# A hybrid decoder block in fp32 on one core: q, k and v leave the projection with channels on partitions, 512 tokens wide, DMAs set q's and k's parts down by head, and the units of mixer A come first

## The chip, the cores and the metric

One core of a Trainium2 chip. The metric is the device time of one execution in microseconds (us). Before the change it was 1175.13 us, the median of three runs (1171.29 to 1176.3).

## What is computed

One decoder layer over 1024 tokens (S) of width 1024 (D), fp32. Cut to what matters here:

```
h = rms_norm(x, g_attn_pre) * (1 + sc_a) + sh_a        # modulation from c @ w_ada
proj = h @ w_in                                        # 1024 -> 2304
qa, ka, va = 512, 128, 128 columns                     # A: 8 q heads, 2 kv heads of 64
qb, kb, vb = 512, 512, 512 columns                     # B: 8 heads of 64
qa, ka, qb, kb = partial_rope(..., cos, sin)           # first 16 of each 64, pairs (i, i+8)
oa = banded_attention(qa, ka, va, 127, sink)           # causal window of 128
ob = dilated_mixture_attention(qb, kb, vb)             # windows (128,1) (512,4) (2048,16)
y = concat(rms_norm(oa), rms_norm(ob)) @ w_out
x = x + gt_a * rms_norm(y, g_attn_post)
x = x + gt_m * rms_norm(sqrelu(h' @ w_up) @ w_down)    # h' from x as h above, 4096 wide
```

## The kernel before, in words

Each fp32 operand of a projection, score or output product is split into two fp32r numbers, hi (a rounded copy, on ScalarE, ACT) and lo (the rest, on VectorE, DVE, or on GpSimd, POOL). A product is three TensorE (PE) matmuls, hi x hi, hi x lo, lo x hi. Transposes are PE matmuls against an identity.

The projection runs in six units of 384 columns of w_in: units 0 to 3 are two B heads each (q, k, v of 128), units 4 and 5 one kv head of A each with its four q heads. For each of eight blocks of 128 tokens, `proj_mm` (L766, L767, L769) keeps a 128 x 128 piece of h (`hw`, hi and lo) as the stationary operand and moves 384 columns of w, over eight k of 128 channels: 48 tiles `pj` of 24 matmuls, tokens on partitions. `evac` (L666 to L758) then works a tile off: v split into hi and lo (L679, L684), the rotation on DVE (L695 to L699), q and k split (`sp`, `sk`, L706 to L712), both transposed by PE through the bank `px` (`pq` L719, `pk` L731), and the transposes copied out by ACT (`qt` L724, `kt` L745, L757). Unit 0 (`first_unit`, L788) has eight accumulators `acc` open at once while x and w_ada still arrive.

Attention goes by items: for B one head of two token blocks (32 items), for A four heads of one block (16). `s_b` (L996) makes a B item's scores `s_ps` in pieces of up to 256 keys (L1022), `s_a_` (L1055) A's (L1073). Masks, maxima, the exponential and its sum follow on DVE and ACT. `t_pv` (L1114) transposes probabilities (`pt_ps`, L1125, L1128, L1132), splits them (`ph`, ACT L1139 and DVE L1143) and multiplies with v into `o_ps` (L1156 to L1167), one PSUM bank `po`. The result `ot` is stored to DRAM (`o_dram`) by SyncE (SP, L1194 for B, L1214 for A). After all items `out_block` reads it back normed and multiplies with w_out (`y_ps`, L1373 to L1375; `load_wo`, L1234, brings and splits w_out). The MLP (`mlp_ps`, L1797 to L1799) follows.

The order on each engine comes from a scheduler in the program (`Sched`, L135): each step has an engine, an estimated duration, what it waits for, which buffers it takes and gives (`Res`), and a priority; steps are placed greedily when they could start. DMAs from SP are such steps, and SP carries them out in the order placed. For PE, `prefer` (L1949) ranks kinds: projection steps ("dense") ahead of attention steps while the projection leads attention by less than `LEAD` = 0.5 unit, behind them otherwise.

## Time and profile before

| what | value |
|---|---|
| median of three runs | 1175.13 us (1171.29 to 1176.3) |
| the profiled execution | 1175.14 us, its span 1173.3 us |
| granted TensorE clock | 0.993 of full speed |
| first transpose of q (unit 0) | 64.6 us |
| first y_ps matmul, first mlp_ps matmul | 436.4 us, 543.9 us |

The recorded lengths of matmuls overlap, since they are pipelined, so the distance from one start to the next is what a stream of them takes. A row such as `x4` stands for four alike in a run. A row of waits names the engine and the tile or line that waited, and after the arrow what released it; then come the sum in us, the number of waits and the longest.

### The profile page before, as it was taken

Reading aid. Unit: us, or ns where it says so; the run is one execution under the profiler, and the core shown is the slowest. Engines: PE = TensorE matmul, PEld = TensorE weight load, DVE = VectorE, ACT = ScalarE, POOL = GpSimd, SP = SyncE. Lnnn points to the kernel's source line nnn. Section 1 sums busy time; section 2 is a strip of 40 time slices with the busy share of each in tenths; the row PEclk is TensorE's granted clock in tenths of the full one; section 3 lists DMA queues with packets and bytes.
Section 4 is the critical chain, followed back from the end, with each engine's and each line's share of the span. In section 5 each row is a group of like instructions: output and inputs, shape, how many; then the busy total and the mean of one; then the engine's idle time right before and its main releaser. Section 6 shows DMA issues by size and latency. Waiting matters only on the chain.

```text
span 1173.3 us, 17394 instructions
## 1 busy us (share of the span) xinstructions
PE 1137.0 (97%) x6042; PEld 987.6 (84%) x6042; DVE 871.9 (74%) x1765; ACT 677.6 (58%) x1421; POOL 239.3 (20%) x295
## 2 busy tenths in 40 slices
PE   8999999999999999999899999999999999999996
PEld 7889999999988878887688888888888888888885
DVE  7876787776788896668969764499653796636998
ACT  7966676666666786666667524473225733246542
POOL 2053464554654451112000000000000000000002
PEclk9999999999999999999999999999999999999998
DMA  9712234132223224465485147922258411575103
GB/s 327 209 64 78 74 87 117 53 104 71 70 70 104 79 73 130 172 202 218 150 333 181 36 150 243 357 84 90 100 214 306 143 50 54 202 283 201 37 19 144
DMA packets 96488, 166.54 MB, mean 142 GB/s; under 512 B 11408, under 2 KB 48400, under 8 KB 96400
## 3 DMA queue, kind: packets, MB, share of 16 engines
q1 hardware_dynamic: 96400, 165.42, 42.0%
q8 instruction: 48, 0.79, 0.3%
q14 instruction: 40, 0.33, 0.1%
HBM read 137.08 MB, written 28.31 MB: 141 GB/s over the span
## 4 chain that ended last, share of the span: by engine, by line
PE 77%; DVE 11%; issue 4%; ACT 3%; POOL 1%; DMA 1%; DVEq 0%; POOLq 0%; SPq 0%; ACTq 0%
PE mlp_ps L1798 16%; PE mlp_ps L1799 16%; PE mlp_ps L1797 16%; PE pj L766 4%; PE pj L767 4%; PE pj L769 4%; PE s_ps L1022 3%; PE o_ps L1156 2%; PE pt_ps L1125 1%; DMA w_st<-in_w_in 1%; PE y_ps L1373 1%; PE y_ps L1375 1%; PE y_ps L1374 1%; PE s_ps L1073 1%; PE pt_ps L1128 1%
## 5 line engine op out<-in xcount | busy, mean ns | idle before, releaser
L1797 PE MATMUL mlp_ps<-hw 128*128 128x512 f32 x896 | 349.7, 390 | 1.1 <-ACT hw L1559 1.1
L1798 PE MATMUL mlp_ps<-hw 128*128 128x512 f32 x896 | 348.7, 389 | 1.1 <-DVE hw L1565 1.1
L1799 PE MATMUL mlp_ps<-hw 128*128 128x512 f32 x896 | 348.6, 389 | 0.0
L1797 PEld LDWEIGHTS mlp_ps<-hw 128*128 128x128 f32 x896 | 168.2, 188 | 36.9 <-ACT hw L1559 1.6
L1798 PEld LDWEIGHTS mlp_ps<-hw 128*128 128x128 f32 x896 | 168.2, 188 | 36.6 <-DVE hw L1565 1.4
L1799 PEld LDWEIGHTS mlp_ps<-hw 128*128 128x128 f32 x896 | 168.2, 188 | 34.9
L1568 DVE TENSOR_TENSOR hw<-w,hw 128x1024 fp32r<-128x1024 f32 x96 | 114.6, 1219 | 95.1 <-ACT hw L1561 93.0
L1561 ACT CAST hw<-w 128x1024 fp32r<-128x1024 f32 x96 | 97.4, 1046 | 129.9 <-PE mlp_ps L1799 93.2
L1897 POOL TENSOR_TENSOR st<-st,nhalf 128x1 f32<-128x1 f32 x8 | 7.7, 977 | 602.0 <-DVE st L1895 602.0
L766 PE MATMUL pj<-w_hl,hw 128*128 128x384 f32 x320 | 119.1, 372 | 0.0
L767 PE MATMUL pj<-w_hl,hw 128*128 128x384 f32 x320 | 108.7, 340 | 0.5 <-DVE w_hl L506 0.5
L769 PE MATMUL pj<-w_hl,hw 128*128 128x384 f32 x320 | 108.9, 340 | 0.0
L1561 ACT CAST hw<-u 128x1024 fp32r<-128x1024 f32 x48 | 48.6, 1052 | 64.6 <-PE mlp_ps L1799 64.6
L1143 DVE TENSOR_TENSOR ph<-pt_ps,ph 128x512 fp32r<-128x512 f32 (+1 forms) x110 | 68.9, 644 | 18.6 <-ACT ph L1139 18.0
L1568 DVE TENSOR_TENSOR hw<-u,hw 128x1024 fp32r<-128x1024 f32 x48 | 57.0, 1218 | 18.2 <-ACT hw L1561 18.2
L1139 ACT CAST ph<-pt_ps 128x512 fp32r<-128x512 f32 (+1 forms) x110 | 59.8, 562 | 12.9 <-PE pt_ps L1128 8.8
L1052 POOL TENSOR_SCALAR p_sb<-p_sb,den 128x128 f32<-128x128 f32 (+3 forms) x64 | 49.1, 773 | 87.4 <-DVE den L1050 49.8
L1855 DVE TENSOR_TENSOR yacc<-yacc,mlp_ps 128x512 f32<-128x512 f32 x96 | 62.2, 681 | 3.3 <-PE mlp_ps L1799 3.3
L767 PEld LDWEIGHTS pj<-w_hl,hw 128*128 128x128 f32 x320 | 61.0, 191 | 2.1 <-DVE w_hl L506 0.8
L766 PEld LDWEIGHTS pj<-w_hl,hw 128*128 128x128 f32 x320 | 60.7, 190 | 1.6 <-issue 0.5
L769 PEld LDWEIGHTS pj<-w_hl,hw 128*128 128x128 f32 x320 | 60.6, 189 | 0.0
L1047 ACT ACTIVATE p_sb<-p_sb,mn 128x128 f32<-128x128 f32 (+3 forms) x64 | 50.0, 782 | 17.4 <-DVE mn L1040 13.5
(206 smaller groups left out, 2201.0 us busy)
## 6 DMA issues: line engine op xcount, KB each, us to landing
hw<-s_dram SPq DMA_DIRECT2D x84, 512.0 KB, 4.4
wa_st<-in_w_ada SPq DMA_DIRECT2D x32, 512.0 KB, 4.2
w<-in_w_up SPq DMA_DIRECT2D x32, 512.0 KB, 5.1
w<-in_w_down SPq DMA_DIRECT2D x32, 512.0 KB, 7.5
s_dram<-hw SPq DMA_DIRECT2D x28, 512.0 KB, 4.5
x_sb<-in_x SPq DMA_DIRECT2D x16, 512.0 KB, 5.4
wa<-in_w_ada SPq DMA_DIRECT2D x32, 256.0 KB, 6.1
w_st<-in_w_in SPq DMA_DIRECT2D x32, 192.0 KB, 3.8
```

The lines of the kernel that those rows point to most:

```text
L766: T.matmul(ps, hw[:, tb, 0, t], w[:, 0], start=(k == 0), stop=False)
L767: T.matmul(ps, hw[:, tb, 0, t], w[:, 1], start=False, stop=False)
L769: T.matmul(ps, hw[:, tb, 1, t], w[:, 0], start=False, stop=(k == KC - 1))
L1047: A.activation(rec.p[qi], rec.p[qi], AF.Exp, bias=b["mn"][:, m:m + 1], scale=-1.0, accum_out=b["den"][:])
L1139: A.copy(b["ph"][:, 0, :w], b["pt"][:, :w])
L1143: V.tensor_tensor(b["ph"][:, 1, :w], b["pt"][:, :w], b["ph"][:, 0, :w].bitcast(F32), ALU.subtract)
L1561: A.copy(out[j][0], flat(src[j]))
L1568: V.tensor_tensor(out[j][1], flat(src[j]), out[j][0].bitcast(F32), ALU.subtract)
L1797: T.matmul(ps[m][:], sh, mh, start=starts and k == 0, stop=False, **kw)
L1798: T.matmul(ps[m][:], sh, ml_, start=False, stop=False, **kw)
L1799: T.matmul(ps[m][:], sl, mh, start=False, stop=k == 3, **kw)
L1855: e = op("DVE", t_dv(512), lambda: V.tensor_tensor(y(), y(), ps[m][:], ALU.add), [e, ml.e_y[tb, n]], gives=gives, prio=1)
```

## The change

**Operands swap in the projection.** w is stationary now, in blocks c = 0, 1, 2 of 128 columns for each unit, and `hw` moves, 512 tokens (x = 0, 1) as four blocks of 128 (L859, L860, L862): 36 tiles `pj` of 128 channels x 512 tokens with 24 matmuls each, 864 of 512 columns for 1152 of 384. The host orders w_in's columns so that c = 0 holds the 16 rotated rows of every q and k head of a unit (and for B nothing else, 128 rows in all), c = 1 more of q and k, c = 2 the rest and v. It comes as 36 tiles of 128 x 512 (L530) in place of 64 pieces (L484).

**Rotation and set-down.** Cos and sin stand in two tables of 128 x 1024 (`tabs`), made by `tables` with POOL fills and copies, PE transposes (`ptab`, L717) and ACT copies, once for A and again ahead of unit 2 for B. Block 0 is rotated by four DVE instructions over 512 tokens. Hi and lo of q and k go to `stage("hl")`, and DMAs on SP (L801) lay each head's 64 rows into `kt` and `qt`, of the one hi above lo, the other twice over: 18 DMAs for each half unit (u, x), 216 in all. The transposes pq and pk, `sp`, `sk` and their copies go; v is copied (`vt`), transposed back by PE in four (`pv`, L829, 48 in all) and split (L837, L840).

**Order.** Units 0 and 1 are A now, 2 to 5 B. LEAD is 0.8. `o_ps` alternates between `po` and `px`. B scores are up to 512 wide (L1120; A's are L1171). Rings hold two units of k (`kt`), two halves of q (`qt`), three of v. w_out's loads start when two projection tiles are left to place, where it was five (tiles then 128 tokens), and the staging buffers grow from three to five. First y_ps lines are L1471 to L1473, probability transposes L1223, L1226, L1230, pv products L1253 to L1265.

PE in the middle of the projection. Before, a B unit:

```order
L766 MATMUL pj<-w_hl,hw 128x384
L767 MATMUL pj<-w_hl,hw 128x384
L769 MATMUL pj<-w_hl,hw 128x384
L719 MATMUL pq<-ident_r,sp 128x128 x2
L766 MATMUL pj<-w_hl,hw 128x384
L767 MATMUL pj<-w_hl,hw 128x384
L769 MATMUL pj<-w_hl,hw 128x384
L766 MATMUL pj<-w_hl,hw 128x384
L767 MATMUL pj<-w_hl,hw 128x384
L769 MATMUL pj<-w_hl,hw 128x384
L731 MATMUL pk<-ident_r,sk 128x128 x4
```

After, in an early unit (`pv` is v's transpose, `o_ps` A's attention):

```order
L859 MATMUL pj<-hw,w_hl 128x512
L860 MATMUL pj<-hw,w_hl 128x512
L862 MATMUL pj<-hw,w_hl 128x512
L829 MATMUL pv<-head,vt 128x128 x4
L1265 MATMUL o_ps<-ph,v_hl 128x512 x2
L859 MATMUL pj<-hw,w_hl 128x512
L860 MATMUL pj<-hw,w_hl 128x512
L862 MATMUL pj<-hw,w_hl 128x512
L1265 MATMUL o_ps<-ph,v_hl 128x512 x2
```

Between the projection's matmuls stood the transposes of q and k; there are now v's, four for a half unit, and attention of A, which before stood beside the last units.

SP, with the semaphores that each row waits for, before: w_in's pieces, a store of attention and w_ada.

```order
L1194 DMA o_dram_113<-ot 64x256 [waits DMAHW5_49,DVE_49]
L484 DMA w_st<-in_w_in 128x3x128 [waits DMAHW6_49,DMAHW0_49,DVE_49]
L484 DMA w_st<-in_w_in 128x3x128 [waits DMAHW7_49,DMAHW1_49,DVE_49]
L896 DMA wa_st<-in_w_ada 128x2x512 [waits Pool_49]
L1194 DMA o_dram_114<-ot 64x256 [waits DVE_49]
```

After: the store, and behind it the set-down of one half unit's block 0, hi first.

```order
L1312 DMA o_dram_110<-ot 64x2x128 [waits DMAHW5_49,DVE_49]
L801 DMA qt<-hl 16x2x512 [waits DMAHW6_49,Activation_49]
L801 DMA qt<-hl 16x2x512 [waits DMAHW7_49]
L801 DMA kt<-hl 16x2x512 [waits DMAHW0_49]
L801 DMA qt<-hl 16x2x512 [waits DMAHW1_49]
L801 DMA qt<-hl 16x2x512 [waits DMAHW2_49]
L801 DMA kt<-hl 16x2x512 [waits DMAHW3_49]
L801 DMA qt<-hl 16x2x512 [waits DMAHW4_49,Pool_49]
```

Behind a store stands a run of set-down DMAs, whose first rows wait for ACT's hi or another engine's lo.

PE from the projection's last matmul, before:

```order
L769 MATMUL pj<-w_hl,hw 128x384
L1132 MATMUL pt_ps<-head,p_sb 128x128 x4
L1073 MATMUL s_ps<-kt,qt 128x256 x8
L1167 MATMUL o_ps<-ph,v_hl 128x512 x2
L1132 MATMUL pt_ps<-head,p_sb 128x128 x4
L1167 MATMUL o_ps<-ph,v_hl 128x512 x2
L1132 MATMUL pt_ps<-head,p_sb 128x128 x4
L1167 MATMUL o_ps<-ph,v_hl 128x512 x4
L1132 MATMUL pt_ps<-head,p_sb 128x128 x8
L719 MATMUL pq<-ident_r,sp 128x128 x4
L1373 MATMUL y_ps<-hw,oh 128x512
```

After (the last unit is of B; pt_ps and s_ps of its items):

```order
L862 MATMUL pj<-hw,w_hl 128x512
L1223 MATMUL pt_ps<-head,p_sb 128x128 x2
L1226 MATMUL pt_ps<-head,p_sb 128x128
L1120 MATMUL s_ps<-kt,qt 128x384 x2
L1120 MATMUL s_ps<-kt,qt 128x512 x2
L1253 MATMUL o_ps<-ph,v_hl 128x256 x2
L1258 MATMUL o_ps<-ph,v_hl 128x256 x2
L1120 MATMUL s_ps<-kt,qt 128x384 x2
L1223 MATMUL pt_ps<-head,p_sb 128x128 x2
L1226 MATMUL pt_ps<-head,p_sb 128x128
```

Before, the first y_ps is ten rows behind the last `pj`; after, 38 more rows of attention stand between the last row shown and the first y_ps (L1471).

The diff, cut:

```diff
--- before.py
+++ after.py
+PARTS_B = (((0, 32, "q", 0), (32, 32, "k", 0), (64, 32, "q", 16), (96, 32, "k", 16)),
+           ((0, 64, "q", 32), (64, 64, "k", 32)), ())
+PARTS_A = (((0, 32, "q", 0), (32, 32, "k", 0), (64, 32, "q", 32), (96, 32, "k", 32)),
+           ((0, 96, "q", 8), (96, 32, "q", 40)), ((0, 64, "q", 48),))
+
...
+    w = h["w_in"][0][:, _columns()].reshape(2, 4, P, 18, P)
+    w = np.ascontiguousarray(w.transpose(3, 0, 2, 1, 4)).reshape(36, P, 512)
+    w[:6] = w[:6].reshape(3, 2, P, 4, P).transpose(2, 1, 3, 0, 4).reshape(P, 6, 512).transpose(1, 0, 2)
+    h["w_in"] = w
...
-    WR, WS, NP, NV, NK, NQ, NT, NO = 10, 5, 4, 21, 10, 12, 2, 6
+    WR, WS, NP, NV, NK, NQ, NT, NO = 6, 2, 4, 3, 2, 2, 2, 4
     r_pj, r_x, r_t, r_s, r_o, r_d = Res(2), Res(1), Res(2), Res(2), Res(1), Res(0)
-    r_stg, r_w, r_wst, r_hl = Res(3), Res(WR), Res(WS), Res(0)
+    r_stg, r_w, r_wst, r_hl = Res(5), Res(WR), Res(WS), Res(0)
     r_u, r_raw, r_h2, r_wo = Res(0), Res(0), Res(0), Res(0)
-    r_sp = Res(2)
+    r_vt = Res(1)
...
-    def load_w(u, k, prio=None, deps=()):
+    def load_w(u, i, prio=None, deps=()):
         def emit():
-            t = w_raw[u, k] = prp.tile([P, UW], F32, name="w_st", tag="w_st", bufs=WS)
-            r = slice(k * P, (k + 1) * P)
...
+            t = w_raw[u, i] = prp.tile([P, 512], F32, name="w_st", tag="w_st", bufs=WS)
+            nc.sync.dma_start(t[:], w_in[6 * u + i])
...
+            w_e[a] = op(("DVE", "POOL"), (t_dv(512), t_ptt(512)), (lo(V), lo(G)), [e], gives=[(r_wst, 1)], prio=3)
...
+    def tables(groups, place, r_place, r_bank, bank, deps):
+        for i in range(2):
+            b = {}
+            def f_rows(i=i, b=b):
+                t = b["t"] = place()[:].rearrange("p (b r) -> p b r", b=TB)
+                G.memset(t, 0.0 if i else 1.0)
+                for o, h in groups:
+                    src = sinw[:, :, 0 if o >= 64 else 1] if i else cosw[:]
+                    G.tensor_copy(t[:, :, o:o + 8 * h].rearrange("p b (r h) -> p b r h", h=h),
+                                  src.unsqueeze(3).to_broadcast([P, TB, 8, h]))
...
+                    for j in range(4):
+                        T.transpose(b[x][:, j], b["t"][:, 4 * x + j], ident)
...
+                e_tab[x].append(op("ACT", t_ps(512) + AP_COST, lambda i=i, x=x, b=b: A.mul(
+                    tabs[i][:, 512 * x:512 * x + 512], b[x][:].rearrange("p b t -> p (b t)"), scl[0]), [d] + deps[x],
+                                   gives=[(r_bank, 1)], prio=2))
...
+    def evac(u, x, c, get_ps, done, r_bank):
+        isb = u > 1
+        parts = (PARTS_B if isb else PARTS_A)[c]
+        cs = slice(512 * x, 512 * x + 512)
         b = {}
...
+        def f_new():
+            b["f"] = stage("hl")[:].rearrange("p (s t) -> p s t", s=2)
+            b["t"] = b["f"].bitcast(F32R)
+        if c == 0:
+            def f_rope():
+                f_new()
+                ps, t = get_ps(), b["f"][:, 1]
+                cos, sin = tabs[0][:, cs], tabs[1]
+                V.tensor_tensor(t[64:128], ps[0:64], sin[0:64, cs], ALU.mult)
+                V.tensor_tensor(t[0:64], ps[64:128], sin[64:128, cs], ALU.mult)
+                V.tensor_tensor(ps[:], ps[:], cos, ALU.mult)
+                V.tensor_tensor(t, t, ps[:], ALU.add)
+            e0 = e_rot[u, x] = op("DVE", 4 * t_dv(512), f_rope, [done] + e_tab[x], takes=[(r_stg, 1)],
+                                  gives=[(r_bank, 1)], prio=2)
+            eh = op("ACT", t_sb(512), lambda: A.copy(b["t"][:, 0], b["f"][:, 1]), [e0], prio=2)
+            def f_lo(eng):
+                return lambda: eng.tensor_tensor(b["t"][:, 1], b["f"][:, 1], b["f"][:, 0], ALU.subtract)
+            el = op(("DVE", "POOL"), (t_dv(512), t_ptt(512)), (f_lo(V), f_lo(G)), [eh], prio=2)
+        elif parts:
+            n = parts[-1][0] + parts[-1][1]
+            sc_ = scl[1] if (isb, c) != (False, 1) else None
+            def f_hi():
+                f_new()
+                A.mul(b["t"][:n, 0], get_ps()[:n], -0.125 if sc_ is None else sc_[:n])
+            def f_lo():
+                V.scalar_tensor_tensor(b["t"][:n, 1], get_ps()[:n], -0.125 if sc_ is None else sc_[:n],
+                                       b["f"][:n, 0], ALU.mult, ALU.subtract)
+            eh = op("ACT", t_ps(512) + AP_COST, f_hi, [done, e_rot[u, x]], takes=[(r_stg, 1)], prio=2)
+            el = op("DVE", t_dv(512) + AP_DV, f_lo, [eh], gives=[(r_bank, 1)] if c < 2 else [], prio=2)
+        if parts:
+            for s_, e_ in ((0, eh), (1, el)):
+                new = c == 0 and s_ == 0
+                def f_st(s_=s_, new=new):
+                    if new:
+                        if not x:
+                            ks[u] = kring.tile([P, 2, 1024], F32R, name="kt", tag="kt")
+                        qs[u, x] = qring.tile([P, 4, 512], F32R, name="qt", tag="qt")
+                    for p0_, n_, whose, row in parts:
+                        src = b["f"][p0_:p0_ + n_, s_]
+                        for i in range(2):
+                            o = 64 * (i if isb == (whose == "q") else s_) + row
+                            if isb != (whose == "q") and i:
+                                continue
+                            if whose == "q":
+                                dst = qs[u, x][:, 2 * s_:2 * s_ + 2] if isb else qs[u, x][:]
+                                nh = 2 if isb else 4
+                            else:
+                                dst = ks[u][:, :, cs] if isb else ks[u][:, s_:s_ + 1, cs]
+                                nh = 2 if isb else 1
+                            nc.sync.dma_start(dst[o:o + n_ // nh].bitcast(F32), src)
...
+                if new:
+                    e_new[u, x] = Ev()
...
+                e = load(f_st, by, [e_] + ([] if new else [e_new[u, x]]), takes=[(r_k, 1 - x), (r_q, 1)] if new else [], prio=-12, n=nd,
+                         gives=[(r_stg, 1)] if s_ else [], after=after)
+                e_q[u, x].append(e)
+                e_k[u, x].append(e)
+        if c < 2:
+            return
+        nh = 2 if isb else 1
+        o = P - 64 * nh
+        def f_vt():
+            b["vt"] = prp.tile([P, 512], F32, name="vt", tag="vt", bufs=1)
+            A.copy(b["vt"][:64 * nh], get_ps()[o:])
+        e = op("ACT", t_ps(512), f_vt, [done] + ([el] if parts else []), takes=[(r_vt, 1)], gives=[(r_bank, 1)], prio=2)
+        def f_pv():
+            b["pv"] = px.tile([P, 4, 64 * nh], F32, name="pv", tag="x")
+            for j in range(4):
+                T.transpose(b["pv"][:, j], b["vt"][:64 * nh, j * P:(j + 1) * P], ident[:64 * nh, :64 * nh])
+        e = pe_op("post", 0.43, f_pv, [e], takes=[(r_x, 1), (r_v, 1)], gives=[(r_vt, 1)])
+        def part(s_):
+            return vs[u, x][:, :, :nh, s_], b["pv"][:].rearrange("p j (h d) -> p j h d", h=nh)
         def f_vh():
+            vs[u, x] = vring.tile([P, 4, 2, 2, 64], F32R, name="v_hl", tag="v")
+            A.copy(*part(0))
         def f_vl():
+            V.tensor_tensor(part(1)[0], part(1)[1], part(0)[0].bitcast(F32), ALU.subtract)
+        e = op("ACT", t_ps(256 * nh), f_vh, [e], prio=2)
+        op("DVE", t_dv(256 * nh), f_vl, [e], gives=[(r_x, 1)], prio=2, after=posted)
...
+
+    def proj_mm(ps, u, c, k, x, part):
+        i, n = w_at(u, c, k)
+        t, w = slice(k * P, (k + 1) * P), w_hl[u, i]
+        n = slice(n * P, n * P + P)
+        h = [hw[:, 4 * x:4 * x + 4, i, t] for i in range(2)]
+        ps = ps[:].rearrange("p (b t) -> p b t", t=P)
         if part != 1:
-            T.matmul(ps, hw[:, tb, 0, t], w[:, 0], start=(k == 0), stop=False)
-            T.matmul(ps, hw[:, tb, 0, t], w[:, 1], start=False, stop=False)
+            T.matmul(ps, w[:, 0, n], h[0], start=(k == 0), stop=False)
+            T.matmul(ps, w[:, 1, n], h[0], start=False, stop=False)
         if part != 0:
-            T.matmul(ps, hw[:, tb, 1, t], w[:, 0], start=False, stop=(k == KC - 1))
+            T.matmul(ps, w[:, 0, n], h[1], start=False, stop=(k == KC - 1))
...
+        order = [(k, part, x, c) for x in range(2) for k in range(2) for part in range(2) for c in range(3)]
+        order += [(k, part, x, c) for k in range(2, AHEAD) for part in range(2) for x in range(2) for c in range(3)]
+        order += [(k, part, x, c) for x in range(2) for c in range(3) for k in range(AHEAD, KC) for part in range(2)]
...
-    todo_dense = [(u, tb) for u in range(6) for tb in range(FIRST if u == 0 else 0, TB)]
+    todo_dense = [(u, x, c) for u in range(1, 6) for x in range(2) for c in range(3)]
...
+            u, x, c = todo_dense.pop(0)
+            if (x, c) == (1, 0):
                 next_unit_w(u)
-            proj_tile(u, tb)
+            if (u, x, c) == (2, 0, 0):
+                for e_ in e_tab:
+                    e_.clear()
+                tables([(0, 2), (32, 2), (64, 2), (96, 2)], lambda: stage("rows"), r_stg, r_x,
+                       lambda: px.tile([P, 4, P], F32, name="ptab", tag="x"), [[e_rot[1, 0]], [e_rot[1, 1]]])
...
-    items = [(u, tp, h) for u in range(4)
-             for tp, h in ((0, 0), (0, 1), (1, 0), (1, 1), (2, 0), (3, 0), (2, 1), (3, 1))]
-    items += [(u, qb) for u in (4, 5) for qb in range(TB)]
-    UB = 2 * (0.218 * 20 + 0.107 * 36 + 0.43 * 10)
+    items = [(u, qb) for u in range(2) for qb in range(TB)]
...
-                    for b0 in range(0, cw, 256):
-                        w = min(256, cw - b0)
-                        for hl in range(2):
-                            T.matmul(s[:, b0:b0 + w], toks[u, qb].q[h][:],
-                                     kts[u, (c0 + b0) // 256, h][:, hl, :w], start=(hl == 0), stop=(hl == 1))
-                d = 0.218 * -(-cw // 256)
-                deps = [toks[u, j].e_k for j in range(2 * tp, 2 * tp + 2)] + [toks[u, qb].e_q]
+                    for hl in range(2):
+                        T.matmul(s[:, :cw], qs[u, qb // 4][:, 2 * hl + h, qb % 4 * P:qb % 4 * P + P],
+                                 ks[u][:, h, c0:c0 + cw], start=(hl == 0), stop=(hl == 1))
+                d = 2 * t_mm(cw)
+                deps = e_k[u, c0 // 512] + e_q[u, qb // 4]
...
-                rec.o = po.tile([P, 512], F32, name="o_ps", tag="o")
+                rec.o = (px if i % 2 else po).tile([P, 512], F32, name="o_ps", tag="x" if i % 2 else "o")
...
-        if len(todo_dense) > 5 or ada.i < NADA:
+        if len(todo_dense) > 2 or ada.i < NADA:
...
-            e = load(f_l, 524288, takes=[(r_stg, 1)], prio=-8)
+            e = load(f_l, 524288, takes=[(r_stg, 1), (r_wo, 1)], prio=-8)
...
-    LEAD = 0.5
+    LEAD = 0.8
```

More of the change, by code (lines that the diff above doesn't have):

```diff
@@ L25 @@
 FF = 4096
-UW = 384
 EPS = 1e-6
@@ L355, in hybrid_block @@
     inv_f = head[:, CW_F:CW_F + 8]
-    ident_r = const.tile([P, P], F32R, name="ident_r")
+    scl = [head[:, CW_SCL + i:CW_SCL + i + 1] for i in range(2)]
     ones = const.tile([P, P], F32, name="ones")
```

317 lines of the change are left out of this document (140 added, 177 removed).

## The prediction

> **What bounds the kernel now.** I read the page's busy shares and chain first, then the stages, then TensorE's own waits, and last the timeline of single matmuls, since a busy share says nothing about how fast a stream of matmuls goes.
>
> The first line of the page's part 1 and the first of the chain that ended last:
>
> ```profile
> PE 1137.0 (97%) x6042; PEld 987.6 (84%) x6042; DVE 871.9 (74%) x1765; ACT 677.6 (58%) x1421; POOL 239.3 (20%) x295
> PE 77%; DVE 11%; issue 4%; ACT 3%; POOL 1%; DMA 1%; DVEq 0%; POOLq 0%; SPq 0%; ACTq 0%
> ```
>
> TensorE (PE) is busy 97% of the span and 77% of the chain. VectorE (DVE) is the only other engine with a share of the chain worth the name. Now the stages; columns are length, then busy time of each engine:
>
> ```profile
> 60.00:436.00 376.00, 362.45 (x2515) 345.88 (x2513) 289.69 (x1014) 255.44 (x812) 195.88 (x233) 0.99 0.28 80
> 360.00:410.00 50.00, 46.33 (x299) 43.79 (x298) 43.61 (x147) 37.07 (x124) 21.38 (x30) 0.97 0.30 94
> L1373 PE MATMUL y_ps<-hw,oh x128: 389/389/497, 436.4 to 543.2; 128*128 128x512 f32 x128
> L1797 PE MATMUL mlp_ps<-hw x896: 389/389/798, 543.9 to 1162.9; 128*128 128x512 f32 x180
> ```
>
> The last two rows say where stages end: the output projection (y_ps) begins at 436.4 us, the MLP at 543.9, and neither is touched by the change. So the whole question is whether the 436.4 us ahead of y_ps get shorter; what is saved there moves the rest forward one for one. From 60 to 436 us TensorE is busy 362.45 of 376 us, VectorE 289.69, ScalarE (ACT) 255.44. VectorE comes near TensorE only where the A heads are worked off (360 to 410: 43.61 against 46.33 of 50). TensorE's waits in that part of the program (us in total, times, longest):
>
> ```profile
> PE pq L719 <- DVE sp L711: 3.7, 3, 2.2
> PE o_ps L1167 <- DVE ot L1207: 2.0, 1, 2.0
> PE pk L731 <- ACT qt L724: 1.2, 2, 0.7
> PE pq L719 <- ACT sk L707: 0.8, 1, 0.8
> PE pt_ps L1125 <- DVE sk L712: 0.4, 1, 0.4
> ```
>
> Waits are few. The time is in the matmuls, so I price them by the distance from one start to the next.
>
> **The change, term by term.**
>
> (a) *Wider projection matmuls.* 1152 of 384 columns become 864 of 512; the columns are the same (442,368), so only a fixed part of each can be saved. The timeline (start us, length us) of the projection and its transposes, then of 512-wide matmuls in the MLP:
>
> ```profile
> 289.33 0.29 PE L719 MATMUL pq<-ident_r,sp 128*128 128x128 f32 x2
> 289.45 0.41 PE L766 MATMUL pj<-w_hl,hw 128*128 128x384 f32 x1
> 289.70 0.34 PE L767 MATMUL pj<-w_hl,hw 128*128 128x384 f32 x1
> ...
> 290.06 0.33 PE L766 MATMUL pj<-w_hl,hw 128*128 128x384 f32 x1
> ...
> 290.58 0.46 PE L731 MATMUL pk<-ident_r,sk 128*128 128x128 f32 x4
> 290.87 0.41 PE L766 MATMUL pj<-w_hl,hw 128*128 128x384 f32 x1
> 291.12 0.33 PE L767 MATMUL pj<-w_hl,hw 128*128 128x384 f32 x1
> ```
>
> ```profile
> 699.62 0.39 PE L1798 MATMUL mlp_ps<-hw 128*128 128x512 f32 x1
> ...
> 700.98 0.39 PE L1798 MATMUL mlp_ps<-hw 128*128 128x512 f32 x1
> ```
>
> From 290.06 to 290.58 three 384-wide steps (two rows left out) take 0.52 us, 0.173 each; from 289.70 to 290.06 two take 0.36, 0.18 each. From 699.62 to 700.98 six 512-wide steps take 1.36 us, 0.227 each. Before: 1152 x 0.173 to 0.180 = 199.3 to 207.4; after: 864 x 0.227 = 196.1. That is -3 to -11 us; I take -6, nearer the quicker row, since it is the undisturbed one. One thing no row shows: the moving operand is now four blocks of 128 columns that lie apart in hw, where every moving operand of before is one piece. I take the same 0.227; each 0.01 us more would cost 8.6 us.
>
> [...]
>
> (b) *The q and k transposes go*: 128 pq and 160 pk. In the same rows two pq take 0.12 us (289.33 to 289.45), four pk 0.29 (290.58 to 290.87): 288 x 0.060 to 0.072 = 17.3 to 20.9 us. The matmul behind each group then takes a longer step: 289.45 to 289.70 and 290.87 to 291.12 are 0.25, which is 0.08 over 0.173. There are 96 such groups (two for each of 48 tiles), 7.7 us. Together -25 to -29; I take -27.
>
> (c) *Waits.* The rows that wait for the old split and transposes (pq, pk, and pt_ps for sk) add up to 6.1 us, that of o_ps for its only bank is 2.0; items now alternate between two banks. A wait that goes may return under another name, so 0 to -8.1; I take -8, and count the new waits in (f) and (g).
>
> (d) *New transposes*: 48 of v and 32 of the cos and sin tables, fp32, in 20 groups of four.
>
> ```profile
> 292.53 0.38 PE L1125 MATMUL pt_ps<-head,p_sb 128*128 128x128 f32 x2
> 292.75 0.38 PE L1128 MATMUL pt_ps<-head,p_sb 128*128 128x128 f32 x2
> ...
> 293.32 0.42 PE L766 MATMUL pj<-w_hl,hw 128*128 128x384 f32 x1
> 293.58 0.34 PE L767 MATMUL pj<-w_hl,hw 128*128 128x384 f32 x1
> ```
>
> Two take 0.22 us (292.53 to 292.75), and the step behind them is 0.26: 80 x 0.11 + 20 x 0.09 = +10.6. Sixteen of v are half as wide, so +8 to +11; I take +10.
>
> (e) *Scores of the B heads*: 320 matmuls become 192, up to 512 wide, over the same columns.
>
> ```profile
> 283.26 0.63 PE L1022 MATMUL s_ps<-kt,qt 128*128 128x256 f32 x4
> 283.74 0.34 PE L766 MATMUL pj<-w_hl,hw 128*128 128x384 f32 x1
> ...
> 285.25 0.33 PE L1022 MATMUL s_ps<-kt,qt 128*128 128x128 f32 x2
> 285.42 0.39 PE L766 MATMUL pj<-w_hl,hw 128*128 128x384 f32 x1
> ```
>
> 256 x 0.12 + 64 x 0.085 = 36.2 us against 32 x (0.085 + 0.12 + 0.173) + 96 x 0.227 = 33.9: -2.
>
> *Beside TensorE.* Work on the projection's results by VectorE and ScalarE leaves the path only where TensorE waited, so it is no term of its own, but it must not grow. The instructions that touch the accumulators of units 1 to 5, and the k transposes (columns as in the stages, without POOL):
>
> ```profile
> 60.00:450.00 390.00, 216.50 (x960) 160.07 (x960) 69.75 (x304) 32.58 (x144) 0.99 0.28 80
> 60.00:450.00 390.00, 20.84 (x160) 18.00 (x160) 12.59 (x32) 20.60 (x62) 0.99 0.28 80
> L1143 DVE TENSOR_TENSOR ph<-pt_ps,ph 128x512 fp32r<-128x512 f32 (+1 forms) x110 | 68.9, 644 | 18.6 <-ACT ph L1139 18.0
> ```
>
> That is 82 us of VectorE and 53 of ScalarE, with unit 0 still to add. After it, VectorE has some 79 instructions of 512 elements (48 of the rotation, 16 and 3 low parts, 12 of v) at 0.65 us from the last row, 51 us; ScalarE has 52. Both fall, so neither becomes the bound on average. Splitting the weights stays: 36 tiles of 512 for 48 of 384, the same elements; their loads become 36 whole tiles for 64 pieces, so SP loses 28 issues there. The tables' fills and copies (20 in all) go to POOL, busy 196 of 376 us; were they late, unit 0's first rotation would wait for them once, a few us. Unit 0 itself has 144 x 0.227 = 32.7 us of matmuls for 192 x 0.173 = 33.2 between the same arrivals of x and w_ada, and I cost its new order at nothing. The A items move to the front: their VectorE work then lies beside four more units of projection, where the cover is TensorE's, and not beside the last one.
>
> (f) *The end of attention.* Before, the last unit is one of A, and small. Now it is a B unit, and the order puts all 72 of its probability transposes behind the last projection matmul. TensorE has there 72 x 0.11 + 84 pv x 0.12 + 40 score matmuls, 7 us + 45 of y_ps x 0.227 = 35 us. VectorE has for the same unit, at 0.65 us per 512 columns: 20 low parts, 13; 24 masked maxima of 384 on average, 12; 8 output adds of 256, 3; and half of w_out's low parts with the first output blocks, six pieces of 1024, 8: 36 us. They are level, so waits are likely: 0 to +12 (a third more than TensorE's own time); I take +3, since two w_out parts or more can go to POOL.
>
> (g) *Setting q and k down.* 216 DMAs, 18 for each of 12 half units (512 tokens of a unit), all issued by SP in order.
>
> ```profile
> L1194 SPq DMA_DIRECT2D o_dram<-ot x32: 445/451/523, 89.0 to 339.8; - x32
> L1214 SPq DMA_DIRECT2D o_dram<-ot x32: 574/578/634, 349.8 to 455.7; - x32
> o_dram<-ot SPq DMA_DIRECT2D x64, 64.0 KB, 2.0
> SPq L1194 <- DVE ot L1191: 136.1, 21, 27.2
> ```
>
> An issue takes 0.45 to 0.58 us and 64 KB land after 2.0: 18 x 0.58 + 2.0 = 12.4 us from a half unit's first high part to its scores. Half units follow each other every 376 / 12 = 31 us, and projection work may run 0.8 of a unit ahead, so most of it lies beside matmuls. All hidden costs 0; all of it bare at 12 places costs 149; by the rows nearest (an SP that mostly waits, TensorE that rarely does) I take +3.
>
> Sum: -6 - 27 - 8 + 10 - 2 + 3 + 3 = **-27 us**. The profiled execution took 1175.14 us (span 1173.3), the median of three is 1175.13, so the forecast is **1148 us**.
>
> **Rivals.** *The end eats it* (f at its far end, +12, and the waits of (c) back under other names for half their size): 1175 - 27 + 9 + 4 = about 1161, up to 1167. For it: 43.61 us of VectorE in 50 where attention alone was left. Against: y_ps is there to fill.
>
> *Gain hidden anyway*: if what TensorE waits for (probabilities through VectorE and ScalarE) set this stage, taking matmuls out would only widen gaps: 1171. Against it stand the short wait rows.
>
> *Slower: set-down stands in SP's queue.* SP holds a store until its data is there, 136.1 us in 21 waits, the longest 27.2, which cost nothing while little stood behind. Now q and k stand behind. If 5 us were bare at 11 half units (55 us in place of 3), the time is 1148 + 52 = 1200; it turns into a loss at (27 + 3) / 11 = 2.7 us each. Against: the lead of 0.8 unit.
>
> [...]
>
> **How the numbers follow.** Forecast (1132 to 1159) 0.60; the end eats it 0.14; hidden 0.10; set-down slower 0.13; the broken-up moving operand at 0.26 or more a step (+28 us, 1176 and above) 0.03. The range 1130 to 1176 leaves out the last two and the rims. A difference under 0.5% (1169 to 1181) can't be told from none: faster 0.76, same 0.08, slower 0.16.
>
> **What would show it.** Right: y_ps starts near 410 us; pj steps of 0.227; no wait rows for pq or pk; waits of s_ps for kt or qt of a few us. Wrong: s_ps waiting for DMAs tens of us (set-down), pj steps over 0.24 (moving operand), o_ps and pt_ps waiting 10 us or more behind the last pj (the end), or VectorE above 90% in the A units, which now come first.

## The result and the profile after

The changed kernel took 1178.06 us (median of seven runs, 1176.76 to 1181.5), the kernel before 1173.84 beside it: a ratio of 1.0042, 95% interval 1.0023 to 1.0062. The forecast was 1148 us. The profiled execution took 1176.76 us.

Part 1's first line of the page after, the chain's, and the two rows that end the stages (first and last start in us):

```profile
PE 1118.5 (95%) x5415; PEld 924.5 (79%) x5415; DVE 845.2 (72%) x1457; ACT 634.8 (54%) x1103; POOL 244.8 (21%) x297
PE 67%; DVE 13%; ACT 6%; issue 5%; DMA 4%; POOL 2%; SPq 2%; DVEq 0%; POOLq 0%; ACTq 0%
L1471 PE MATMUL y_ps<-hw,oh x128: 388/390/482, 429.7 to 544.9; 128*128 128x512 f32 x128
L1895 PE MATMUL mlp_ps<-hw x896: 388/390/799, 545.6 to 1164.6; 128*128 128x512 f32 x180
```

TensorE is busy 18.5 us less, and the MLP starts at 545.6 where it started at 543.9. TensorE's share of the chain fell from 77% to 67%; what came in is VectorE, ScalarE, DMA and SP's queue. The longest waits of TensorE after, in the order of the view:

```profile
PE pv L829 <- ACT vt L823: 9.7, 2, 7.8
PE s_ps L1171 <- DMA kt<-hl: 5.5, 1, 5.5
PE o_ps L1265 <- DVE ph L1241: 4.8, 4, 2.5
...
PE o_ps L1253 <- DVE ph L1241: 3.3, 5, 1.3
PE s_ps L1171 <- DMA qt<-hl: 2.3, 1, 2.3
```

To see work and waits apart, I took every distance from one matmul's start to the next, up to the MLP, from both timelines, and gave each shape a step price: 0.227 us for 512 columns, 0.173 for 384, 0.117 for 256, 0.109 for a 128-wide fp32 transpose, 0.059 for other 128-wide matmuls, 0.112 for a single column, 0.060 for the 64-wide pv. What a distance has beyond its price counts as a wait if it is over 0.15 us, as slow steps if it is less. So a step of 0.43 us at the lower clock (last section) counts as a wait too: 22.8 us of the waits before and 45.9 after stand where the profile names a wait, 8.9 and 12.5 where it names none.

| us up to the MLP | before | after |
|---|---|---|
| priced steps | 481.0 | 467.3 |
| slow steps | 29.6 | 18.3 |
| waits over 0.15 us | 31.8 | 58.4 |
| sum, with the first start at 1.5 | 543.9 | 545.6 |

**The work fell by 25.0 us, and the waits rose by 26.6.** The wider projection step is what the MLP's rows promised; undisturbed, 19 steps from 72.57 to 76.89 take 0.227 us each, so four blocks of 128 columns that lie apart cost nothing here:

```profile
72.57 0.39 PE L859 MATMUL pj<-hw,w_hl 128*128 128x512 f32 x1
...
76.89 0.39 PE L860 MATMUL pj<-hw,w_hl 128*128 128x512 f32 x1
```

Where the waits are shows in three stretches after (length, then PE, PEld, DVE, ACT, POOL busy, granted clock, DMA share, GB/s):

```profile
60.00:100.00 40.00, 30.27 (x150) 24.75 (x149) 19.87 (x62) 19.14 (x55) 14.08 (x19) 0.91 0.63 152
100.00:205.00 105.00, 96.44 (x516) 77.57 (x515) 93.96 (x264) 69.01 (x190) 60.46 (x83) 0.99 0.58 148
205.00:225.00 20.00, 12.20 (x58) 9.84 (x57) 7.02 (x18) 7.62 (x17) 12.83 (x15) 0.86 0.67 158
```

In the first and the last of them no engine is full. They are the two places where set-down stands in the way, and the last shows how far it reaches. ScalarE, SP and TensorE there:

```profile
210.11 0.48 ACT L1237 CAST ph<-pt_ps 128x384 fp32r<-128x384 f32 x1 [0.91 <-PE pt_ps L1226]
218.59 0.62 ACT L539 CAST w_hl<-w_st 128x512 fp32r<-128x512 f32 x1 [8.00 <-DMA w_st<-in_w_in]
...
221.22 0.59 ACT L823 COPY vt<-pj 128x512 f32<-128x512 f32 x1
```

```profile
198.04 1.26 SPq L1312 DMA_DIRECT2D o_dram<-ot  x2
199.40 1.25 SPq L801 DMA_DIRECT2D qt<-hl  x2
...
214.13 0.60 SPq L801 DMA_DIRECT2D kt<-hl  x1
214.78 1.07 SPq L530 DMA_DIRECT2D w_st<-in_w_in  x2
```

```profile
213.66 0.40 PE L862 MATMUL pj<-hw,w_hl 128*128 128x512 f32 x1
221.86 1.12 PE L829 MATMUL pv<-head,vt 128*128 128x128 f32 x4 [7.80 <-ACT vt L823]
```

SP issues the 18 set-down DMAs of a half unit from 199.40 to 214.7 (2.8 us of that it waits for block 0's low part from GpSimd), and only then the next weight tile's load. ScalarE's next instruction in order is that tile's cast: it stands 8.0 us, with v's copy behind it, and TensorE's next in order is v's transpose. No scores waited here. The issue itself (shortest, median, longest in ns, first and last start):

```profile
L801 SPq DMA_DIRECT2D qt<-hl x136: 542/592/2135, 66.8 to 407.3; - x136
L801 SPq DMA_DIRECT2D kt<-hl x80: 507/590/1162, 67.7 to 408.5; - x80
```

### The profile page after: what moved, and what is told of

It is laid out like the page before. It is cut to its first block, busy times and chain, and to the rows that moved or that the text cites. A ratio compares the mean times of both kernels' runs of the same rounds, so it can differ in the third digit from the quotient of the medians.

```text
span 1175.0 us, 15811 instructions
## 1 busy us (share of the span) xinstructions
PE 1118.5 (95%) x5415; PEld 924.5 (79%) x5415; DVE 845.2 (72%) x1457; ACT 634.8 (54%) x1103; POOL 244.8 (21%) x297
## 4 chain that ended last, share of the span: by engine, by line
PE 67%; DVE 13%; ACT 6%; issue 5%; DMA 4%; POOL 2%; SPq 2%; DVEq 0%; POOLq 0%; ACTq 0%
PE mlp_ps L1896 16%; PE mlp_ps L1897 16%; PE mlp_ps L1895 16%; SPq L801 2%; PE pj L859 2%; PE pj L860 2%; PE pj L862 2%; PE s_ps L1120 2%; DVE ph L1241 1%; PE o_ps L1253 1%; PE acc L876 1%; DMA o_sb<-o_dram 1%; DVE hw L1666 1%; PE y_ps L1473 1%; PE y_ps L1471 1%
## 5 line engine op out<-in xcount | busy, mean ns | idle before, releaser
L859 PE MATMUL pj<-hw,w_hl 128*128 128x512 f32 x240 | 104.2, 434 | 0.0
L860 PE MATMUL pj<-hw,w_hl 128*128 128x512 f32 x240 | 95.5, 398 | 0.0
L862 PE MATMUL pj<-hw,w_hl 128*128 128x512 f32 x240 | 95.5, 398 | 0.0
L1008 POOL TENSOR_TENSOR ada_acc<-ada_acc,wa_st 128x512 f32<-128x512 f32 x42 | 55.2, 1314 | 3.5
L862 PEld LDWEIGHTS pj<-hw,w_hl 128*128 128x128 f32 x240 | 45.7, 190 | 10.5
L1471 PE MATMUL y_ps<-hw,oh 128*128 128x512 f32 x128 | 51.2, 400 | 0.0
```

Of the source, the lines that this page charges most:

```text
L859: T.matmul(ps, w[:, 0, n], h[0], start=(k == 0), stop=False)
L860: T.matmul(ps, w[:, 1, n], h[0], start=False, stop=False)
L862: T.matmul(ps, w[:, 0, n], h[1], start=False, stop=(k == KC - 1))
L1471: T.matmul(ps[:], b["oh"][:, k], wh[:, c0:c0 + 512], start=(k == 4 * m), stop=False)
```

## The experiments

Three theories stood: **1**, the count of issues in a row on SP; **2**, work of VectorE and ScalarE that sets the pace, with A in front and B at the end; **3**, the transfers themselves, onto few partitions. One thing decides how a run is read. The scheduler writes a new order on every engine whenever one of its inputs changes, and a new order alone can move the time by several us (9 us in s5_land, below). Three runs leave its inputs as they were (s2_split, t6, t18), so the instructions of TensorE, VectorE, ScalarE and GpSimd come in the changed kernel's order, and these runs measure a cost; the others measure a cost together with a new order.

### Twice the issues, in the same order (s2_split)

```diff
-    nc.sync.dma_start(dst[o:o + n_ // nh].bitcast(F32), src)
+    for t_ in (0, 256):
+        nc.sync.dma_start(dst[o:o + n_ // nh, :, t_:t_ + 256].bitcast(F32), src[:, t_:t_ + 256])
```

> The changed kernel with every set-down DMA cut in two by tokens: 432 DMAs of half the bytes, the order on all engines as it was. Theory 1 (number of issues on SP): 216 x 0.6 = 130 us more of SP between 65 and 410 us, of which SP's own holds cover a part: 1200 to 1260 us. Theory 2 (VectorE and ScalarE): 1176 to 1182. Theory 3 (transfers, same bytes): 1176 to 1185.

1297.94 us, ratio 1.1046 (1.1006 to 1.1086). SP's rows:

```profile
L802 SPq DMA_DIRECT2D qt<-hl x272: 542/594/1709, 66.3 to 528.1; - x136
L802 SPq DMA_DIRECT2D kt<-hl x160: 547/590/1758, 67.9 to 529.4; - x160
```

Half the bytes, the same 0.59 us: here the price is one per DMA. 216 more at 0.59 are 127 us, and the time rose by 120 over the changed kernel's 1178, nearly all of it bare; theory 1 had expected 1260 at most. Of the three theories only the first expects a loss of this kind. It says what more issues cost, not what the first 216 do; the next two runs ask that.

### Whole tiles, in the same order (t6 and t18)

Each block goes into qt and kt as it stands, so the scores are of other numbers. The third block of an A unit, which holds q's last rows, sends nothing.

```diff
+    src = b["f"][:, s_, t0:t1]          # t6: 0 to 512; t18: 0, 192, 384, 512
+    nc.sync.dma_start(qs[u, x][:, 2 * c + s_, t0:t1].bitcast(F32), src)
+    if c == 0:
+        nc.sync.dma_start(ks[u][:, s_, 512 * x + t0:512 * x + t1].bitcast(F32), src)
```

> The changed kernel with the order of every engine as it was, but q and k are not laid down by head: each block's 128 channels are copied as they stand into qt and kt, whole tiles on 128 partitions, 6 DMAs a half unit in place of 18, about the same bytes; so the scores are of other numbers. Theory 1 (issues in a row on SP) and theory 3 (transfers onto few partitions) both expect the waits at 77 to 97, at 213.7 and half of those behind the last projection matmul to go: 1145 to 1158 us. Theory 2 (VectorE and ScalarE set the pace, and the waits come back under other names): 1170 to 1180.

> As the run with 6 whole-tile DMAs a half unit, but each cut in three by tokens: 18 DMAs a half unit as in the changed kernel, of a third of the size, on 128 partitions; the scores are of other numbers here too. Theory 1 (count of issues): near the changed kernel, 1172 to 1180 us. Theory 3 (few partitions): near the run with 6, 1145 to 1158. Theory 2: 1172 to 1180.

t6: 1156.15 us, ratio 0.9851 (0.9822 to 0.9879). t18: 1167.45, ratio 0.9949 (0.9933 to 0.9964). The changed kernel, with the same order, is at 1178.06. So **set-down by head costs 22 us over set-down as whole tiles**: 11.3 between 6 and 18 DMAs of one form, 10.6 between 18 on 128 partitions and 18 on 8 to 32. t6 lies where theories 1 and 3 expected it, below theory 2's 1170 to 1180. t18 lies between the ranges of 1 and 3, so both the count and the form seem to matter. t6's set-down rows on SP and its three stretches, to be held against those of the changed kernel:

```profile
L793 SPq DMA_DIRECT2D qt<-hl x48: 464/488/1308, 66.7 to 374.5; - x48
L795 SPq DMA_DIRECT2D kt<-hl x24: 473/596/857, 67.3 to 371.6; - x24
```

```profile
60.00:100.00 40.00, 37.42 (x202) 31.06 (x201) 32.06 (x98) 27.54 (x80) 22.50 (x30) 0.98 0.59 208
100.00:205.00 105.00, 100.23 (x535) 81.91 (x534) 89.05 (x250) 68.55 (x183) 67.78 (x87) 0.98 0.51 159
205.00:225.00 20.00, 20.00 (x118) 17.30 (x117) 14.00 (x35) 10.13 (x20) 11.69 (x12) 1.00 0.44 139
```

TensorE is busy 37.42 of the first 40 us (30.27 before this edit) and all of the last 20. The waits over 0.15 us by stretch, in the same way as above:

| us | changed | t18 | t6 |
|---|---|---|---|
| up to 60 | 6.6 | 6.0 | 6.2 |
| 60 to 100 | 12.8 | 5.9 | 3.5 |
| 100 to 205 | 12.9 | 11.0 | 8.7 |
| 205 to 225 | 9.5 | 8.7 | 0.0 |
| 225 to the MLP | 16.6 | 15.9 | 17.7 |
| sum | 58.4 | 47.5 | 36.1 |

From 60 to 100 us the waits fall mostly with the form, from 205 to 225 with the count: t18 still has the wait for v's copy, t6 has not.

```profile
PE pv L823 <- ACT vt L817: 6.6, 1, 6.6
```

The form shows in the landings. Those of set-down by head are counted from the updates of the DMAs' semaphores in the trace: nine for a DMA onto 8 partitions, thirteen onto 24, sixteen onto 16, 32 or 128. Counted so, no update is left over. From issue to landing, 64 KB take at the least 1.91 us onto 128 partitions (t18), 2.21 onto 16 and 2.94 onto 8 (the changed kernel); the median of all set-down DMAs is 2.0 us in t18 and 2.95 in the changed kernel.

One thing more differs, so the 10.6 us aren't the form's alone. A score of A in the changed kernel needs the last of its half unit's 18 DMAs, since every q DMA brings a few rows of all its heads; in t18 it needs only the pieces of its own slot of qt. Six of t18's first eight scores start before the last of the 18 is issued, at 78.29 us:

```profile
77.58 0.89 PE L1165 MATMUL s_ps<-kt,qt 128*128 128x128 f32 x6
79.04 0.44 PE L1165 MATMUL s_ps<-kt,qt 128*128 128x128 f32 x2 [0.58 <-DMA qt<-hl]
```

That last DMA landed at 80.2, so even scores that waited for all 18 could have started some 5 us ahead of the changed kernel's, which start at 85.38. What the fewer waits are worth elsewhere, no run shows.

### Relief for SP, with a new order (s1_pack, s4_wq, q_act)

s1_pack sends hi and lo of what lies twice in one DMA (216 to 152). s4_wq has ScalarE issue the weight loads of units 1 to 5, q_act has it issue all low parts (edits cut to the line that matters):

```diff
-    src = b["f"][p0_:p0_ + n_, s_]                                                  # s1_pack
+    src = b["f"][p0_:p0_ + n_] if dup else b["f"][p0_:p0_ + n_, s_]
+    (nc.sync if u == 0 else nc.scalar).dma_start(t[:], w_in[6 * u + i])             # s4_wq
+    (nc.scalar if s_ else nc.sync).dma_start(dst[o:o + n_ // nh].bitcast(F32), src) # q_act
```

> The changed kernel, but hi and lo of an operand that lies twice over go in one DMA: 152 set-down DMAs in place of 216, the same bytes. Theory 1 (SP's queue: the number of issues in a row, 0.59 to 0.73 us each, holds up scores, staging buffers and weight loads): SP has 38 us less to issue, the waits of TensorE from 60 to 100 us (12.8 us) lose about a quarter and the 8 us one at 213.7 about half, so 1168 to 1173 us. Theory 2 (attention's own work on VectorE and ScalarE sets the pace once TensorE has less to do): no change, 1176 to 1180. Theory 3 (the transfers themselves, bytes onto few partitions): no change either, 1176 to 1180.

> The changed kernel with the weight loads of units 1 to 5 (30 DMAs) issued by ScalarE's queue and not behind the set-down on SP. Theory 1: the 8 us wait at 213.7 (ScalarE held at a weight tile's cast until its load landed) goes, 1167 to 1171 us; 30 issues of some 0.5 us on ScalarE cost nothing that shows. Theory 2: no change or slower, 1176 to 1186, since ScalarE has 15 us more. Theory 3: no change, 1176 to 1180.

> The changed kernel with the set-down of all low parts (108 DMAs) issued by ScalarE's queue in place of SP's; bytes, order of units and all else as changed. Theory 1 (SP's issues in a row): half of the run stands beside the other half, the waits at 77 to 97, at 213.7 and behind the last projection matmul shrink by half or more, 1158 to 1170 us. Theory 2 (VectorE and ScalarE set the pace): ScalarE has 65 us more, 1180 to 1200. Theory 3 (transfers): no change, 1175 to 1181.

1177.54, 1194.33 and 1189.51 us; ratios 1.0030 (1.0014 to 1.0046), 1.0169 (1.0126 to 1.0211), 1.0135 (1.0090 to 1.0179). All three miss what theory 1 expected. s1_pack took what theories 2 and 3 expected, q_act lies in theory 2's range (ScalarE has more to do there), s4_wq in nobody's; each has a new order, so none of them decides between the theories. The waits moved: s4_wq's two longest single ones are

```profile
PE pv L833 <- DVE gate_st L1042: 8.0, 1, 8.0
...
PE s_ps L1175 <- DMA kt<-hl: 4.4, 1, 4.4
```

The wait at 213.7 is gone there, and one of the same length stands elsewhere; the waits add up to 74.7 us (q_act 70.0, s1_pack 58.2). In these three runs, taking load off SP didn't help while the order was laid out anew by the same prices.

### Lead and w_out (l12, f_wo)

LEAD 1.2 for 0.8; and w_out's loads without r_wo, from four tiles left. In f_wo w_out's halves land in hw while the last projection tiles still read it, so the last columns are of other numbers.

```diff
-    LEAD = 0.8                                                # l12
+    LEAD = 1.2
-    e = load(f_l, 524288, takes=[(r_stg, 1), (r_wo, 1)], prio=-8)   # f_wo
+    e = load(f_l, 524288, takes=[(r_stg, 1)], prio=-8)
```

> The changed kernel with LEAD 1.2 in place of 0.8: projection may run further ahead of attention. Theory 1: more time between a half unit's high part and its scores, so 1168 to 1174 us, unless the two buffers for halves of q hold the lead where it was (1175 to 1180). Theory 2: VectorE has the same work in the same stretch, 1175 to 1182.

> The changed kernel, but w_out's loads may start two projection tiles sooner and needn't wait for the last weight tiles to be used. Theory 1 for the end (w_out's loads stand behind the last 18 set-down issues on SP, 394.9 to 409.2 us, so that y_ps can't fill the gaps between 409 and 430): the waits of 9.8 us shrink by half, 1171 to 1175 us. Theory 2 for the end (VectorE and ScalarE are level with TensorE there whatever stands ready): 1176 to 1180. If the loads take staging buffers that set-down needs: 1180 to 1190.

1196.26 (ratio 1.0193, 1.0162 to 1.0224) and 1186.28 (1.0112, 1.0083 to 1.0141). Both ranges for l12 ended below that: more lead made waits, not cover (75.4 us of them). f_wo lies where it was expected if w_out's loads take buffers from set-down, but it doesn't settle its question: its waits up to the MLP are 63.3 us, and 4.8 of them are projection matmuls that wait for the overwritten hw.

### The scheduler's price for set-down (s3_price, s5_land, s6_packprice)

The scheduler counts 0.48 us for an issue (`0.48 * o.n`), and the trace shows 0.59 and more. s3_price counts 1.35 times as much for set-down; s5_land also has it land 2.5 us later; s6_packprice is s1_pack with the price.

```diff
-    prio=-12, n=nd,
+    prio=-12, n=1.35 * nd,
+    ev[0].t += 2.5          # s5_land, in the step's after()
```

> The changed kernel, but the scheduler counts 1.35 times the 0.48 us that it has for one set-down issue, 0.65 us, near the 0.59 to 0.73 of the trace. Theory 1: the order puts other work where the waits stood, so TensorE's waits from 60 to 225 us (35 us) shrink by a third or so: 1165 to 1174 us. Theories 2 and 3: nothing that waits is moved, 1175 to 1181.

> The changed kernel; the scheduler counts 0.65 us for a set-down issue and has each set-down land 2.5 us later than it thought. Theory 1 with the price as what is wrong (an order laid out for quicker set-down): no worse than the run with 0.65 alone (1174), better if landing counts, 1164 to 1174 us. Theory 2: 1174 to 1182.

> The changed kernel with hi and lo of what lies twice in one DMA (152 in place of 216) and 0.65 us for an issue in the scheduler. Theory 1: both help, 1162 to 1171 us. Theory 2: 1173 to 1180.

1174.05 (1.0011, 0.9992 to 1.0030), 1168.62 (0.9958, 0.9942 to 0.9974), 1168.63 (0.9962, 0.9943 to 0.9980). s3_price ends at the upper rim of theory 1's range, the other two inside theirs. s5_land issues the same 216 DMAs and is 9 us under the changed kernel: nothing but the order differs. The wait at 213.7 is gone in all three (205 to 225 us: 1.2, 1.7 and 2.0 us).

### The order of the units (o1_blast, o2_blast_land, o3_blast_v, s9_afirst_v)

B's four units first, then A's two, with the set-down and the widths of the change; o1_blast with the old price, o2_blast_land with s5_land's.

```diff
-    if u > 1:                                   # B
+    if u < 4:                                   # and alike wherever A and B part
-    items = [(u, qb) for u in range(2) for qb in range(TB)]
+    items = [(u, tp, h) for u in range(4) ...] + [(u, qb) for u in (4, 5) for qb in range(TB)]
```

> The changed kernel with the units back in the old order: four of B first, the two of A last; set-down, widths and banks as changed. Theory 1 (SP's issues): the first set-down still stands bare and its weight loads still stand behind it, 1172 to 1180 us. Theory 2 (A's items, rich in VectorE work, cost more in front, and a B unit costs more at the end): TensorE's waits from 100 to 205 us (12.9) fall to the 4.4 that the kernel before has there, and those from 405 to 460 (9.8) to its 4.6, so 1161 to 1168 us.

> The changed kernel with B's units first and A's last, and the scheduler's prices for issue and landing as in the run with both (1168.6 with A first). If A first is a gain of its own (11 us in the run without the prices), it is slower than that run by about as much: 1176 to 1184 us. If the 11 us were only the wrongly priced set-down, which B units have more of at the end: 1165 to 1172.

o1_blast: 1189.51 us (1.0145, 1.0105 to 1.0185), slower than either theory expected, and I took A first for a gain of 11. o2_blast_land: **1154.40 us (0.9833, 0.9813 to 0.9853)**, 14 under A first at the same price and 19 under the kernel before. The expectation had 1165 at best. Its first four rows of waits, and the row that starts the MLP:

```profile
PE o_ps L1267 <- DVE v_hl L842: 4.7, 1, 4.7
PE px L1536 <- ACT xn L1527: 3.6, 2, 3.1
PE o_ps L1255 <- DVE ph L1243: 2.5, 4, 1.7
PE s_ps L1173 <- DVE mn L1188: 2.4, 2, 1.5
...
L1897 PE MATMUL mlp_ps<-hw x896: 387/389/798, 522.0 to 1141.9; 128*128 128x512 f32 x180
```

No row of TensorE's waits names set-down any more; its waits up to the MLP are 34.1 us, near the 31.8 of before, and the MLP starts 21.9 us sooner than there. From 60 to 100 us it has 0.3 us of waits, from 100 to 205 5.4. Whether that was a lucky order, the pair with both prices moved (1.25 times and 2.0 us) was to tell:

> B's units first, as in the run that took 1154.4 us, with the scheduler's two prices for set-down moved a little: 0.60 us for an issue and 2.0 us for the landing in place of 0.65 and 2.5. If B first with honest prices is what brings the time down, it stays near: 1152 to 1162 us. If 1154.4 was a lucky order that any small change of the prices upsets: 1165 to 1185.

> A's units first, the changed kernel's order, with the same moved prices, 0.60 and 2.0 us (1168.6 us with 0.65 and 2.5). If A first is worse by 14 us whatever the prices: 1165 to 1175 us. If the orders differ by luck only, it may fall on either side of the run beside it.

o3_blast_v 1164.97 (0.9929, 0.9905 to 0.9953), s9_afirst_v 1171.76 (0.9984, 0.9966 to 1.0002). The first falls between the two ranges, at the rim of the one for a lucky order. The three pairs together:

| prices for issue and landing | A first | B first |
|---|---|---|
| 0.48 us, nothing more | 1178.06 | 1189.51 |
| 0.60 us, 2.0 us more | 1171.76 | 1164.97 |
| 0.65 us, 2.5 us more | 1168.62 | 1154.40 |

With either pair of raised prices B first is ahead, and faster than the kernel before; with the old price it is behind. Some 10 us lie between the two runs with B first and raised prices. How much of that is the price and how much the luck of an order, these runs can't tell.

### All three edits, and more lead (s7_all, s8_all_l10)

Pack, price and landing together; and the same with LEAD 1.0.

```diff
-    prio=-12, n=nd,         # on s1_pack
+    prio=-12, n=1.35 * nd,
+    ev[0].t += 2.5
-    LEAD = 0.8              # s8_all_l10
+    LEAD = 1.0
```

> The changed kernel with all three edits: hi and lo of what lies twice in one DMA (152 in place of 216), 0.65 us for an issue and 2.5 us more for the landing in the scheduler. If count of issues and the scheduler's prices are separate causes, their gains add to some degree: 1160 to 1168 us. If they are one cause (the order only has to leave room), it stays at the 1168.6 that each pair gave: 1167 to 1171.

> As the run with all three edits, with LEAD 1.0 in place of 0.8. If what still waits is scores for set-down, more lead hides more of it: 1156 to 1166 us. If the lead was slower before (1196 at 1.2) because the two halves of q hold it up and the work of VectorE bunches, slower here too: 1172 to 1185.

1175.64 (1.0013, 0.9998 to 1.0028) and 1187.02 (1.0110, 1.0085 to 1.0134), the first outside both its ranges, the second 2 us above the slower one. The gains don't add, and more lead is slower here too. Why pack takes s5_land's gain back isn't settled: up to 225 us both have 31 us of waits (s7_all 30.7, s5_land 31.9), and s7_all has more behind the last projection matmul (13.1 from 405 to 460, against 10.6).

## Why the prediction was wrong

**(a), (b), (d), (e), the work of TensorE: right.** By the table's sums of priced and slow steps, projection matmuls went from 229.6 to 223.0 (-6.6; forecast -6, and part of (b)'s steps behind a group are in here), 22.8 us of pq and pk are gone (-27 with those steps), pv and ptab add 7.8 (+10), scores went from 55.1 to 52.4 (-2.7; -2). All work together is -25.0, and these four terms of the forecast sum to -25. That they meet so closely is luck: (a) and (b) gave 3.6 less than forecast, (d) cost 2.2 less, and the rest lies in (e) and in other matmuls. The rival of a slow moving operand fell with the 0.227.

**(c), waits that go, -8: wrong.** They came back under other names, even where set-down is cheap: t6 has 36.1 us of waits to before's 31.8.

**(f), the end, +3: small, near what was taken.** From 225 us to the MLP the changed kernel waits 16.6 us; the kernel before waits 15.3 from 200 us on. From 405 to 460 us, around the end of the projection, it is 9.8 against 5.6. So "the end eats it" fell, at least at this price.

**(g), set-down, +3: the step that failed.** The forecast took +3 of a range to 149 "by the rows nearest (an SP that mostly waits, TensorE that rarely does)". With the order held fixed it is 22 us against whole tiles. Three things in that step were off. The issue was 0.59 where 0.45 to 0.58 was taken, which is little. The landing was taken from 64 KB stores, 2.0 us, where the median is 2.95; half of the 22 us goes when the same count of DMAs writes whole tiles of 128 partitions. And the cover was judged for scores alone, "from a half unit's first high part to its scores": what stood bare at 213.7 was a weight tile behind the run, with ScalarE's whole queue behind the tile. The forecast's own view of half units every 31 us averaged over a stage in which the first two half units come at once, and there the first scores of A stand bare for 5.5 us. They start at 85.38 us, 18.5 us behind the first set-down DMA at 66.84, where 12.4 were worked out: the eighteenth DMA is issued only at 79.81, and by its semaphore's updates it landed at 85.33, 5.5 us later (the last row names a kt DMA of the next half unit, which had updates in the same moment).

```profile
66.84 0.84 SPq L801 DMA_DIRECT2D qt<-hl  x1
...
79.81 0.59 SPq L801 DMA_DIRECT2D qt<-hl  x1
...
85.38 1.97 PE L1171 MATMUL s_ps<-kt,qt 128*128 128x128 f32 x8 [5.48 <-DMA kt<-hl]
```

The rival "set-down stands in SP's queue" named the place and the price of turning, 2.7 us for each of eleven half units. About 2 were bare on average (22 / 11), in a few large pieces. With (c), (f) and (g) the forecast had -2 us of waits; t6 has +4.3, so 6 more, and set-down by head 22 on top: 1148 + 6 + 22 = 1176, the profiled execution's 1176.76. The rival's 1200 was too much, but its mechanism, with a chance of 0.13, is the one that the runs show. Beside the queue the form seems to count: the shortest landings of 64 KB, 2.21 us onto 16 partitions and 2.94 onto 8 in the changed kernel, are 0.3 and 1.0 us longer than t18's 1.91 onto 128.

What stood outside all of the forecast's rivals: **A first**. It was written off as "the cover is TensorE's". From 100 to 205 us VectorE is busy 93.96 of 105 us after, just under the 90% that the forecast named as a sign, and TensorE waits 12.9 us there, 8.7 even in t6. But the runs don't show that VectorE's load is the cause. With B first VectorE has much less to do in that stretch, and TensorE waits 5.4 us in o2_blast_land (first row) and still 12.1 in o3_blast_v:

```profile
100.00:205.00 105.00, 102.20 (x592) 86.01 (x591) 72.86 (x198) 60.97 (x134) 78.82 (x85) 1.00 0.64 174
100.00:205.00 105.00, 96.96 (x557) 82.33 (x557) 68.92 (x179) 54.32 (x118) 71.80 (x75) 0.98 0.62 160
```

B first was 14 and 7 us ahead at the raised prices and 11 behind at the old one. So what the order of the units is worth by itself, and why, stays open.

## What to carry to other kernels

The DMAs that replaced compute here had a price in their issuer's queue (0.59 us each on SP, the median), and what stood behind them in that queue was late with them (the weight tile behind 18 of them, for which ScalarE stood 8.0 us): list what stands behind the run (weight loads, stores), not only who reads its result. Where a written scheduler lays out every engine's order, a new kind of step needs its price from a trace first; here the same change is 1178 us with a guessed 0.48 us, 1168.6 with 0.65 and a later landing, and 1154.4 with the units in the old order besides (1189.5 in that order with the guessed price). To measure what a step costs, hold the order fixed and change only the step; a run with a new order measures luck too, perhaps up to 10 us here.

## What the runs showed of the hardware

The time to issue a DMA from SP hardly depended on its size: 0.59 us median for the set-down, whole or cut in two, and for whole tiles of 256 KB 0.49 to qt and 0.60 to kt. It depended more on the form: among the set-down DMAs the median is 0.72 us onto 8 partitions and 0.59 onto 16.

The wait of 5.5 us that ends at 85.38 cost more than its length, since TensorE came back slow, with 4 us at half speed behind it. A 512-wide step takes 0.43 us there until about 89.4, and 0.23 from 90.62; the granted clock is 0.50 from 85.4 to 89.4 us and 1.00 from 90.6 to 96. Behind the wait of 7.8 us that ends at 221.86 it is 0.50 until 226 and 1.00 from 226 to 230.

```profile
87.68 0.63 PE L860 MATMUL pj<-hw,w_hl 128*128 128x512 f32 x1
88.10 0.63 PE L862 MATMUL pj<-hw,w_hl 128*128 128x512 f32 x1
88.53 0.63 PE L859 MATMUL pj<-hw,w_hl 128*128 128x512 f32 x1
...
90.62 0.39 PE L859 MATMUL pj<-hw,w_hl 128*128 128x512 f32 x1
90.85 0.40 PE L860 MATMUL pj<-hw,w_hl 128*128 128x512 f32 x1
```
